# TensorE's work in the order of emission, with estimated pauses between a mixer's steps

## The chip, the cores and the metric

The kernel runs on one core of a Trainium2 chip. The metric is the device time of one execution in microseconds (us), the median of three runs. The engines are TensorE (PE in the rows; its weight loads are PEld), VectorE (DVE), ScalarE (ACT), GpSimd (POOL) and SyncE (SP), which issues the DMAs.

## What is computed

Two sequences of 512 tokens go through two layers of an encoder. In each layer four mixers work side by side on parts of one projection, and their normalised outputs are joined by a second one:

```
def encoder_trunk(x, p):
    for l in range(DEPTH):
        h = rms_norm(x, p['ln1_g'][l]).astype(x.dtype)
        z = h @ p['w_in'][l]
        z_s5, z_hy, z_rw, z_na = jnp.split(z, IN_SPLITS, axis=-1)
        y_s5 = s5_mixer(z_s5, ...)
        y_hy = hyena_mixer(z_hy, ...)
        y_rw = rwkv_mixer(z_rw, ...)
        y_na = na_mixer(z_na, ...)
        groups = [rms_norm(y, p['grp_g'][l, i]).astype(x.dtype) for i, y in enumerate((y_s5, y_hy, y_rw, y_na))]
        x = x + jnp.concatenate(groups, axis=-1) @ p['w_out'][l]
        h = rms_norm(x, p['ln2_g'][l]).astype(x.dtype)
        x = x + jnp.square(jax.nn.relu(h @ p['w_mlp1'][l])) @ p['w_mlp2'][l]
    return x
```

The model width is 1024, the hidden width 4096. S5 is a state-space scan in 16 groups; Hyena is two long convolutions by Fourier transforms (forward products, a product of spectra, inverse products); RWKV is a delta-rule recurrence over both directions, worked in chunks of 64 tokens; the attention looks at 8 rows by 16 columns around each token.

## The kernel before

**Dense products.** A layer l of sequence b has `w_in` (22 tiles of 128 output channels), `w_out` (8), `mlp1` (32) and `mlp2` (64 halves of a tile's sum). Each product is made with its operands split in a high and a low part, as three matmuls of 128x512 columns (`mm3`, L1433 high by high, L1434 high by low, L1435 low by high). One weight piece of 256 KB (4 x 128 x 128) serves 12 matmuls; there are 9024 dense matmuls in all. `load_w` brings a piece: the first time the raw weights come by DMA, ScalarE casts the high part (L300), VectorE subtracts to get the low part (L301, both in `split`), and a DMA stores the low part; for the second sequence high and low come by DMA and ScalarE casts (L1417). There are seven buffers for weight pieces' parts; a first-time piece uses one of three for the high part and one of four for the low.

**Mixers.** Each mixer is a generator that yields between its steps. RWKV has two `rw_step` calls for each (l, b), one for each group of chunks. In each, for the two halves c of the channels, small products (L413) give decay and gate, some twenty elementwise instructions on ScalarE, VectorE and GpSimd make from them the operands of the pair products (L470), whose last ones are L453 and L454. Then come transposes (L506), an inversion on VectorE (L515, L516, L533 to L551), 32-row products (L564, L583), and four tail steps (L640, L650, L661, L676, L678), in which VectorE writes the state `rw_st` and GpSimd multiplies it by the decay into `rw_se` (L668). Hyena has forward products (L1227), a product of spectra on VectorE (L1196 among others) and inverse products (L1277), twice. S5's state products are L959 and L1014. Norms take column sums (L271), a reciprocal root on VectorE and transposes that spread it (L289, L296).

**Order.** `together` steps three generators in turn: the dense stream, the RWKV stream and a first stream for the head, two mixer steps for each dense step. A dense step is one whole tile of 24 matmuls. RWKV and S5 of one (l, b) run side by side, then Hyena and attention. This order of emission gives priorities; a scheduler, which plays the instructions through a timeline of its own, puts them in each engine's order, with the dense products at a lower priority (`OFF_P`). So a mixer's product whose operands are not ready is passed by dense products on TensorE. The mixers of one (l, b) lie beside the dense layers of the one before it. `w_out` of an (l, b) needs all four mixers; in the head, (0, 0) has no earlier layer to run beside. PSUM has 2 banks for dense products (`pd`), 3 for `ra` (RWKV, Hyena), 2 for `ma` and 1 for `nm`.

## Time and profile before

| what | value |
|---|---|
| median of three runs | 3193.9 us (3186.03 to 3196.83) |
| profiled execution | 3182.62 us |
| its span | 3180.8 us |
| TensorE busy | 2964.7 us, 93% of the span |
| VectorE busy | 1935.5 us, 61% |
| ScalarE busy | 1128.3 us, 35% |
| GpSimd busy | 453.6 us, 14% |

Shares are averages over the whole span. A window shows the busy time of each engine and the granted TensorE clock of one stretch. The idle time before a group of instructions tells how long its engine stood still just ahead of them, and the name after `<-` tells what ended the wait.

### The profile page before, as it was taken

How to read it: one execution, taken by the hardware profiler on the slowest of the kernel's cores; microseconds unless marked ns; L12 is line 12 of the kernel's file. 1: busy time of each engine (PE TensorE's matmuls, PEld its weight loads, DVE VectorE, ACT ScalarE, POOL GpSimd, SP SyncE). 2: the span in 40 equal slices, each digit the busy share in tenths (PEclk: the TensorE clock that was granted, in tenths of full speed). 3: DMA queues.
4: the chain of work that ended last, by engine and by line, in shares of the span. 5: the costliest groups of instructions: out<-in, count | busy, mean ns of one | idle time of the engine just before them, and what ended most of it. 6: DMA issues, size and time to landing. Idle time of an engine off the chain costs nothing. (4 is left out here: it accounts for less than half of the span.)

```text
span 3180.8 us, 48627 instructions
## 1 busy us (share of the span) xinstructions
PE 2964.7 (93%) x17328; PEld 2317.7 (73%) x17328; DVE 1935.5 (61%) x3909; ACT 1128.3 (35%) x2080; POOL 453.6 (14%) x411
## 2 busy tenths in 40 slices
PE   7978999899999999999999899988999999799999
PEld 5666776677777867777777677866777777588887
DVE  7987783874874697653844527668547467731223
ACT  4333233443332343244332324333433333343332
POOL 3422210200100022211101002213000001100000
PEclk9988997899999999999999999989999999899999
DMA  7577564464565566774764655666646555466666
GB/s 220 184 228 189 172 188 142 139 169 158 163 194 168 188 204 202 240 236 155 207 174 145 182 169 196 218 200 187 177 139 169 174 178 185 155 215 194 194 192 215
DMA packets 491801, 588.70 MB, mean 185 GB/s; under 512 B 188678, under 2 KB 239494, under 8 KB 490536
## 3 DMA queue, kind: packets, MB, share of 16 engines
q1 hardware_dynamic: 491560, 585.59, 60.1%
q8 instruction: 139, 2.28, 0.3%
q14 instruction: 102, 0.84, 0.1%
HBM read 418.34 MB, written 164.22 MB: 183 GB/s over the span
## 5 line engine op out<-in xcount | busy, mean ns | idle before, releaser
L1433 PE MATMUL pd<-m,m 128*128 128x512 f32 x2984 | 1222.0, 410 | 63.8 <-ACT m L300 23.4
L1435 PE MATMUL pd<-m,m 128*128 128x512 f32 x2984 | 1205.7, 405 | 22.5 <-DMA m<-lo 15.7
L1434 PE MATMUL pd<-m,m 128*128 128x512 f32 x2984 | 1205.8, 404 | 1.6 <-DVE m L301 1.4
L1433 PEld LDWEIGHTS pd<-m,m 128*128 128x128 f32 x2984 | 578.3, 194 | 214.2 <-ACT m L300 27.8
L1435 PEld LDWEIGHTS pd<-m,m 128*128 128x128 f32 x2984 | 577.9, 194 | 166.3 <-DMA m<-lo 19.5
L1434 PEld LDWEIGHTS pd<-m,m 128*128 128x128 f32 x2984 | 579.1, 194 | 131.2 <-issue 8.4
L300 ACT CAST m<-m 128x512 fp32r<-128x512 f32 (+1 forms) x400 | 256.4, 644 | 619.9 <-PE pd L1434 220.6
L1417 ACT CAST m<-m 128x512 fp32r<-128x512 f32 x376 | 232.2, 619 | 612.9 <-DMA m<-in_w_mlp 362.4
L301 DVE TENSOR_TENSOR m<-m,m 128x512 fp32r<-128x512 f32 (+1 forms) x400 | 303.1, 761 | 203.4 <-ACT m L300 198.1
L1596 DVE TENSOR_TENSOR m<-pd,m 128x512 f32<-128x512 f32 x224 | 153.9, 688 | 205.4 <-PE pd L1435 204.5
L1578 DVE SCALAR_TENSOR_TENSOR do<-pd,do 128x512 f32<-128x512 f32 x128 | 88.0, 687 | 202.4 <-ACT do L1577 201.9
L1196 DVE TENSOR_TENSOR m<-m,m 128x512 f32<-128x512 f32 (+1 forms) x224 | 125.6, 601 | 6.5 <-PE ma L1375 4.8
L301 DVE TENSOR_TENSOR m<-do,m 128x512 fp32r<-128x512 f32 x128 | 88.2, 689 | 50.0 <-ACT m L300 49.2
L300 ACT CAST m<-do 128x512 fp32r<-128x512 f32 x128 | 79.4, 621 | 98.7 <-DVE do L1578 98.5
L1577 ACT ACTIVATE do<-pd 128x512 f32<-128x512 f32 x128 | 75.9, 593 | 37.6 <-PE pd L1435 37.3
L668 POOL TENSOR_TENSOR rw_se<-rw_st,rw_ec 128x256 f32<-128x256 f32 x24 | 15.8, 659 | 484.1 <-DVE rw_st L669 361.9
L470 PE MATMUL ra<-m,m 64*128 64x128 f32 x512 | 63.1, 308 | 21.8 <-DVE m L454 10.3
L1196 POOL TENSOR_TENSOR m<-m,m 128x512 f32<-128x512 f32 x32 | 49.0, 1534 | 234.7 <-DVE m L1196 77.7
L1457 POOL TENSOR_TENSOR m<-m 128x512 f32<-128x512 f32 x40 | 59.8, 1494 | 152.9 <-ACT m L1456 150.9
L863 POOL TENSOR_TENSOR m<-m,s5p_i 128x256 f32<-128x256 f32 x64 | 61.7, 963 | 135.7 <-DVE m L865 71.4
L678 PE MATMUL ra<-m,m 128*64 128x64 f32 x512 | 78.8, 248 | 1.3 <-DVE m L653 0.9
L470 PEld LDWEIGHTS ra<-m,m 64*128 64x128 f32 x512 | 54.3, 206 | 34.9 <-issue 24.3
(363 smaller groups left out, 3505.6 us busy)
## 6 DMA issues: line engine op xcount, KB each, us to landing
m<-in_w_mlp SPq DMA_DIRECT2D x512, 256.0 KB, 2.9
lo<-m SPq DMA_DIRECT2D x376, 256.0 KB, 2.6
m<-lo SPq DMA_DIRECT2D x376, 256.0 KB, 2.7
m<-in_w_in SPq DMA_DIRECT2D x176, 256.0 KB, 3.2
m<-zr SPq DMA_DIRECT2D x36, 512.0 KB, 4.8
m<-in_w_out SPq DMA_DIRECT2D x64, 256.0 KB, 3.5
m<-in_xT SPq DMA_DIRECT2D x32, 256.0 KB, 4.3
zr<-do SPq DMA_DIRECT2D x32, 256.0 KB, 2.4
```

The lines of the kernel that those rows point to most:

```text
L300: self.nc.scalar.copy(out=hi, in_=x)
L301: eng.tensor_tensor(out=lo, in0=x, in1=hi.bitcast(F32), op=SUB)
L470: nc.tensor.matmul(out=pm[q][:, ch - c2, c], lhsT=bk[c][h, ch].rearrange("p a b -> p (a b)"), rhs=ar[c][h, ch].rearrange("p a b -> p (a b) ...
L678: nc.tensor.matmul(out=py[b0:b0 + 64, d, c], lhsT=uv[:, ch, c, q], rhs=sr[:, ch, 2 * c + q], start=st is None, stop=True)
L1196: eng.tensor_tensor(out=o, in0=a, in1=b, op=op)
L1417: nc.scalar.copy(out=hi, in_=raw)
L1433: K.nc.tensor.matmul(out=ps, lhsT=wh, rhs=hh, start=(i == 0), stop=False)
L1434: K.nc.tensor.matmul(out=ps, lhsT=wh, rhs=hl, start=False, stop=False)
L1435: K.nc.tensor.matmul(out=ps, lhsT=wl, rhs=hh, start=False, stop=(i == n - 1))
L1577: nc.scalar.activation(out=r, in_=ps, func=AF.Relu)
L1578: nc.vector.scalar_tensor_tensor(out=r, in0=ps, scalar=0.0, in1=r, op0=MAX, op1=MUL)
L1596: nc.vector.tensor_tensor(out=a, in0=ps, in1=a, op=ADD)
```

## The change

All matmuls and transposes go through a helper `K.pe`, which adds an estimated duration to a clock of its own for each. A mixer's `yield N` now says in how many estimated us its next step can begin. `pace` takes the place of `together`: it steps each mixer whose time has come, then one dense step, which is now half a tile (12 matmuls); when nothing moved the clock, it moves it by 0.5. From the first `w_out` on (`(0, 0, "out")`) TensorE executes in the order of emission; the scheduler places the other engines as before. Norms become generators with pauses; the norm of `w_in` and `mlp` is spread between the first dense tiles, whose results wait in PSUM (`early`). RWKV's tail steps, attention's `values` and Hyena's transposes yield more often. Attention starts at the tail of the second `rw_step`, and Hyena right after RWKV, so that three mixers can run at once; their memory may use a further region. Of first-time weights three low parts in four are subtracted on GpSimd. The number of matmuls of each kind stays the same.

```diff
+class PE:
+
+
+    def __init__(self, nc):
+        self.nc, self.clock = nc, 0.0
+
+    def matmul(self, out, lhsT, rhs, **kw):
+        n = int(np.prod(rhs.shape[1:]))
+        self.clock += n * (0.00044 if rhs.dtype == F32R else 0.00168)
+        self.nc.tensor.matmul(out=out, lhsT=lhsT, rhs=rhs, **kw)
+
+    def transpose(self, out, x, eye):
+        self.clock += 0.11
+        self.nc.tensor.transpose(out, x, eye)
...
         if square:
             nc.vector.reciprocal(out=x, in_=x)
-            return x
-        return self.rsqrt(x, n, tag)
-
-    def head_bcast(self, rn, M, tag):
+            y = x
+        else:
+            y = self.rsqrt(x, n, who)
+        yield 4.5
+        return y
+
+    def head_bcast(self, rns, M, tag, use):
 
         nc = self.nc
-        ex = M([P, 4, 2, 64])
-        nc.scalar.copy(out=ex, in_=rn.unsqueeze(3).to_broadcast([P, 4, 2, 64]))
-        pb = self.p([P, S], tag)
-        for q in range(4):
-            nc.tensor.transpose(pb[:, q * P:q * P + P], ex[:, q].rearrange("p a b -> p (a b)"), self.eye)
-        M.free(ex)
-        return pb
+        exs = []
+        for rn in rns:
+            ex = M([P, 4, 2, 64])
+            nc.scalar.copy(out=ex, in_=rn.unsqueeze(3).to_broadcast([P, 4, 2, 64]))
+            exs.append(ex)
+        yield 2.5
+        for c, ex in enumerate(exs):
+            pb = self.p([P, S], tag)
+            for q in range(4):
+                self.pe.transpose(pb[:, q * P:q * P + P], ex[:, q].rearrange("p a b -> p (a b)"), self.eye)
+            use(c, pb)
+            M.free(ex)
...
         bk.append(b_t)
-        yield
+        yield (2, 11)[c]
...
             wt = K.t([P, 2, 2, 64], "rw_wt")
             nc.vector.tensor_tensor(out=wt, in0=pw, in1=wv[:, sl], op=ADD)
+            yield 2
...
         Z = [z0, z1, a, Y[0]]
-        yield
+        yield 9
...
-        values(c, 0, s0, vt)
-        yield
+        yield 9
+        yield from values(c, 0, s0, vt)
         if c == 0:
             a = yield from project(1)
-        values(c, 2, s1, vt)
+        yield 4
+        yield from values(c, 2, s1, vt)
         M.free(vt)
-        yield
+        yield 2
...
-        K.split(hi, lo, raw, nc.vector)
+        K.split(hi, lo, raw, nc.vector if K.nw % LO_V == 0 else nc.gpsimd)
...
 def dense(K, key, h, tag="pd"):
 
-    w = [load_w(K, key + (kh,)) for kh in range(2)]
     ps = K.p([P, S], tag)
-    mm3(K, ps, [(w[k // 4][0][:, k % 4], w[k // 4][1][:, k % 4], h[k][0], h[k][1]) for k in range(8)])
+    for kh in range(2):
+        wh, wl = load_w(K, key + (kh,))
+        mm3(K, ps, [(wh[:, j], wl[:, j]) + h[4 * kh + j] for j in range(4)], kh == 0, kh == 1)
+        if kh == 0:
+            yield
     return ps
...
-def norm_rstd(K, st, M, square=False):
-
-    K.tc.cur_priority -= OFF_R
-    rn = K.token_rstd([st["acc"]], S, K.ones[:, 0:1], 1e-6, "nm", sc=1.0 / D, square=square)
+def norm_rstd(K, st, M, out, square=False):
+
+    yield
+    rn = yield from K.token_rstd([st["acc"]], S, K.ones[:, 0:1], 1e-6, "nm", "nm", sc=1.0 / D, square=square)
     M.free(st['mem'])
     pb = K.p([P, S], "nm")
     K.bcast(rn, pb)
     r = K.t([P, S], "R")
     K.nc.scalar.copy(out=r, in_=pb)
-    K.tc.cur_priority += OFF_R
-    return r
-
-
-def w_in(K, l, par, h, R, dst, tags):
+    out.append(r)
+
+
+def w_in(K, l, par, h, st, M, dst, tags):
 
     nc = K.nc
     zr, zd, zh, zn = dst
+    Rs = []
+    rs = norm_rstd(K, st, M, Rs)
+    next(rs)
...
+    R, early = None, []
     for off, n, fn in ((8, 8, rw), (0, 2, s5), (2, 6, hy), (16, 6, na)):
         for i in range(n):
-            fn(i, dense(K, ('w_in', l, off + i), hp, tags.pop() if tags else "pd"))
+            ps = yield from dense(K, ('w_in', l, off + i), hp, tags.pop() if tags else "pd")
+            if R is None:
+                next(rs, None)
+                early.append((fn, i, ps))
+                if Rs:
+                    R = Rs[0]
+                    for f, j, p in early:
+                        f(j, p)
+            else:
+                fn(i, ps)
             yield
...
-        first(f)
+        yield from first(f)
+        next(rs, None)
         yield
...
-    def __init__(self, gen, n=1, off=0):
-        self.gen, self.n, self.off, self.live = gen, n, off, True
+    def __init__(self, gen):
+        self.gen, self.live, self.ready = gen, True, 0.0
 
     def step(self, K):
-        for _ in range(self.n):
-            if self.live:
-                K.tc.cur_priority += self.off
-                try:
-                    next(self.gen)
-                except StopIteration:
-                    self.live = False
-                K.tc.cur_priority -= self.off
-
-
-def together(K, *streams):
-
-    for _ in both(K, *streams):
-        pass
+        try:
+            self.ready = K.pe.clock + (next(self.gen) or 0.0)
+        except StopIteration:
+            self.live = False
 
 
 def both(K, *streams):
 
     while any(s.live for s in streams):
         for s in streams:
-            s.step(K)
-        yield
+            if s.live and s.ready <= K.pe.clock:
+                s.step(K)
+        yield max(0.0, min([s.ready for s in streams if s.live], default=0.0) - K.pe.clock)
+
+
+def pace(K, dense, ordered, *mixers):
+
+
+    region = None
+    while dense.live or any(s.live for s in mixers):
+        now = K.pe.clock
+        n = 0
+        for s in mixers:
+            if s.live and s.ready <= now:
+                s.step(K)
+                n += 1
+        if dense.live:
+            dense.step(K)
+        if K.pe.clock == now:
+            K.pe.clock += 0.5
+        if region is None and ordered():
+            region = K.tc.manual_schedule(engines={mybir.EngineType.PE})
+            region.__enter__()
+    if region is not None:
+        region.__exit__(None, None, None)
...
-        DM, MX = K.mem((0, DHI)), K.mem((DHI, NMEM))
+        DM, MX, MN = K.mem((0, DHI)), K.mem((DHI, NMEM), (0, DHI)), K.mem((DS5, NMEM), (DHI, DS5), (0, DHI))
         DS, MW = K.mem((0, DLO)), K.mem((DLO, DHI), (DHI, NMEM))
-        MR, MS = K.mem((DHI, DS5), (DS5, NMEM), tight=True), K.mem((DS5, NMEM), (DHI, DS5))
+        MR, MS = K.mem((DHI, DS5), (DS5, NMEM), (0, DHI), tight=True), K.mem((DS5, NMEM), (DHI, DS5), (0, DHI))
...
+                if i >= 15:
                     done.add(("zr", l, b))
-                    if b == 0 and l and len(ys[l - 1, 1]) == 4:
-                        take(l - 1, 1)
-                    if b == 1 and l and len(ys[l, 0]) == 4:
-                        take(l, 0)
+                    other = (l, 0) if b else (l - 1, 1)
+                    if l and len(ys[other]) == 4 and other not in taken:
+                        take(*other)
...
+                done.add((l, b, "out"))
...
-                yield from both(K, Stream(rwkv(l, b, MR)), Stream(chain(until(("z", l, b)), s5(l, b, MS))))
+                K.b = b
+                yield from both(K, Stream(rwkv(l, b, MR)), Stream(chain(
+                    until(("z", l, b), ("ops", l)), s5(l, b, MS), s5_ops(K, 1, MS, "ma") if i == 1 else (),
+                    until(("tail", l, b), ("freed",) + before) if i else (), na(l, b, MN, "ma") if i else ())),
+                    Stream(chain(until(("rw", l, b), ("freed",) + before), hyena(l, b, MX, "ra")) if i else chain()))
                 if i:
-                    yield from until(("freed",) + before)
-                    yield from both(K, Stream(hyena(l, b, MX, "ra")), Stream(na(l, b, MX, "ma")))
                     if i == 1:
-                        yield from prep(1, MX, "ma")
+                        yield from hy_spectra(K, 1, MX, "ma")
...
-        together(K, Stream(first_stream(), FN, OFF_M), Stream(rwkv_stream(), MIX), Stream(ds, 1, OFF_D))
+        pace(K, Stream(ds), lambda: (0, 0, "out") in done, Stream(first_stream()), Stream(rwkv_stream()))
...
-OFF_D, LO_V, MIX = 0, 4, 2
-FN, OFF_M, OFF_W, OFF_P, OFF_R = 2, 0, 0, 2000, 0
+LO_V, OFF_W, OFF_P = 4, 0, 2000
```

`K.mem` with more regions takes the later ones only when the earlier are full. `manual_schedule` fixes the order of the engines it names within its region.

**The end of the mixers on TensorE.** These rows stand ahead of the last `w_out`, in the kernel before; `ra` and `ma` are banks of the mixers, `pd_25377` is the first tile of `w_out`, and the last dense product of the preceding layer stands twelve rows ahead of the first row here, with 28 more L1277 products between.

```order
L1277 MATMUL ra_22905<-m_22100,m_22771 128x128
L1277 MATMUL ra_22916<-m_22100,m_22771 128x128
L296 MATMUL ma_22764<-c_eye_129,rsq_yma_22752 128x128 x4
L271 MATMUL ra_22979<-c_ones_131,m_22974 128x1 x4
L296 MATMUL ra_22998<-c_eye_129,rsq_yra_22986 128x128 x4
L1433 MATMUL pd_25377<-m_25351,m_25365 128x512
```

In the changed kernel the same place, from the last products of the preceding layer (`pd_25309`) to `w_out` (`pd_25367`); L203 is the helper's matmul, L207 its transpose:

```order
L203 MATMUL pd_25309<-m_25022,m_25301 128x512 x2
L203 MATMUL pd_25309<-m_25022,m_25302 128x512
L203 MATMUL pd_25309<-m_25083,m_25301 128x512 x2
L203 MATMUL pd_25309<-m_25083,m_25302 128x512
L203 MATMUL ra_25326<-c_ones_131,m_25244 128x1 x4
L207 MATMUL ra_25346<-c_eye_129,rsq_yra_25333 128x128 x4
L203 MATMUL pd_25367<-m_25353,m_25368 128x512 x2
```

The Hyena inverse (L1277) and the transposes of its neighbour's norm are no longer behind the last dense product; one norm's sums and transposes are.

**RWKV's preparation on TensorE.** In the kernel before, `m_13725` and `m_13726` are the operands of the first half, `m_13769` and `m_13770` those of the second. Between the second half's first products (L413) and these rows stand 20 dense products, three L470 products of the first half, and 35 more dense products, of which the last ones are shown:

```order
L1434 MATMUL pd_17641<-m_14040,m_17629 128x512
L1435 MATMUL pd_17641<-m_14040,m_17630 128x512
L1433 MATMUL pd_17641<-m_14152,m_17629 128x512
L1434 MATMUL pd_17641<-m_14152,m_17629 128x512
L470 MATMUL ra_13831<-m_13769,m_13770 128x128
L470 MATMUL ra_13832<-m_13769,m_13770 128x128
L470 MATMUL ra_13831<-m_13725,m_13726 128x128
L470 MATMUL ra_13832<-m_13725,m_13726 128x128
```

In the changed kernel `m_15277` is an operand of the first half, `m_15345` of the second. Between the second half's L413 products and these stand 48 dense products, of which the last are shown:

```order
L203 MATMUL pd_15401<-m_13823,m_15420 128x512 x2
L203 MATMUL pd_15401<-m_13823,m_15421 128x512
L203 MATMUL pd_15401<-m_13888,m_15420 128x512 x2
L203 MATMUL pd_15401<-m_13888,m_15421 128x512
L203 MATMUL ra_15446<-m_15277,m_15278 128x128
L203 MATMUL ra_15447<-m_15277,m_15278 128x128
L203 MATMUL ra_15446<-m_15345,m_15346 128x128
L203 MATMUL ra_15447<-m_15345,m_15346 128x128
```

The pair products of both halves now come together, with 48 dense products between the second half's first products and them instead of 55.

**The tail of a `rw_step` on GpSimd.** In the kernel before, three `rw_se` stand one behind the other, then come the instructions of the next step:

```order
L668 TENSOR_TENSOR rw_se_20015<-rw_st_19970,rw_ec_19062 128x256
L668 TENSOR_TENSOR rw_se_20109<-rw_st_20013,rw_ec_19062 128x256
L668 TENSOR_TENSOR rw_se_20163<-rw_st_20107,rw_ec_19062 128x256
L430 MEMSET m_20253 128x8x2
L442 TENSOR_TENSOR m_20260<-m_20226,m_20253 128x8x64
```

In the changed kernel L699 is that instruction, and L326 is the subtraction for a weight piece's low part (`m_21130` and so on):

```order
L699 TENSOR_TENSOR rw_se_21099<-rw_st_20974,rw_ec_19276 128x256
L326 TENSOR_TENSOR m_21130<-m_21131,m_21129 128x512
L326 TENSOR_TENSOR m_21172<-m_21173,m_21171 128x512
L699 TENSOR_TENSOR rw_se_21245<-rw_st_21097,rw_ec_19276 128x256
L326 TENSOR_TENSOR m_21276<-m_21277,m_21275 128x512
L326 TENSOR_TENSOR m_21310<-m_21311,m_21309 128x512
L326 TENSOR_TENSOR m_21376<-m_21377,m_21375 128x512
L699 TENSOR_TENSOR rw_se_21408<-rw_st_21243,rw_ec_19276 128x256
```

Between one `rw_se` and the next there now stand two or three subtractions for weights.

## Rows read from the trace of the kernel before

**Rows 1.** The page, busy us of each engine, share of the span, instructions:

```profile
PE 2964.7 (93%) x17328; PEld 2317.7 (73%) x17328; DVE 1935.5 (61%) x3909; ACT 1128.3 (35%) x2080; POOL 453.6 (14%) x411
```

**Rows 2.** Windows: length, busy us (x) of PE, PEld, DVE, ACT, POOL, clock, DMA:

```profile
0.00:590.00 590.00, 524.86 (x3332) 396.31 (x3333) 443.21 (x1001) 211.90 (x395) 150.62 (x146) 0.89 0.63 185
590.00:1420.00 830.00, 774.00 (x4625) 608.15 (x4624) 566.47 (x1125) 301.32 (x560) 128.06 (x115) 0.97 0.62 190
1420.00:2780.00 1360.00, 1271.17 (x7639) 987.83 (x7638) 816.98 (x1629) 479.20 (x896) 168.45 (x146) 0.95 0.58 178
2100.00:2200.00 100.00, 81.23 (x492) 66.33 (x491) 84.66 (x203) 31.20 (x54) 28.89 (x20) 0.85 0.63 199
2700.00:2800.00 100.00, 78.74 (x378) 61.50 (x377) 66.51 (x128) 32.02 (x63) 10.48 (x8) 0.88 0.52 167
2900.00:3000.00 100.00, 100.00 (x441) 82.51 (x440) 25.34 (x39) 32.42 (x55) 0.00 (x0) 1.00 0.61 195
```

**Rows 3.** TensorE's groups by line, 590 to 2780 us: busy, mean ns, idle before:

```profile
L1433 PE MATMUL pd<-m,m 128*128 128x512 f32 x2056 | 845.2, 412 | 41.3 <-DVE do L1578 13.8 <-ACT m L300 6.9 <-ACT m L1417 6.4
...
L470 PE MATMUL ra<-m,m 64*128 64x128 f32 x384 | 48.0, 310 | 19.1 <-DVE m L454 10.3 <-DVE m L453 5.8 <-POOL m L454 2.7
...
L1277 PE MATMUL ra<-m,m 128*128 128x128 f32 x192 | 26.4, 293 | 10.6 <-DVE m L1196 10.5
...
L959 PE MATMUL ma<-m,m 128*64 128x64 f32 x384 | 20.8, 244 | 11.7 <-DMA m<-s_sB 11.7
```

**Rows 4.** TensorE's waits, 590 to 2780 us: total us, times, longest:

```profile
PE ra L564 <- DVE m L551: 18.1, 6, 4.4
```

**Rows 5.** TensorE's timeline at the mixers' end: start, duration, line, [idle before <-releaser]:

```profile
2748.99 0.95 PE L271 MATMUL ma<-c_ones,m 128*128 128x1 f32 x8
2758.25 5.63 PE L1277 MATMUL ra<-m,m 128*128 128x128 f32 x32 [8.31 <-DVE m L1196]
...
2770.18 1.86 PE L271 MATMUL ra<-c_ones,m 128*128 128x1 f32 x8 [5.86 <-DVE m L1534]
2774.18 1.08 PE L296 MATMUL ra<-c_eye,rsq_yra 128*128 128x128 f32 x4 [2.13 <-DVE rsq_yra L257]
2777.92 1.22 PE L1433 MATMUL pd<-m,m 128*128 128x512 f32 x2 [2.65 <-ACT m L300]
```

**Rows 6.** TensorE's timeline, RWKV's first products and pair products, shortest and longest of six:

```profile
1733.78 1.32 PE L413 MATMUL ra<-m 64*128 64x256 f32 x12
...
1750.92 1.57 PE L470 MATMUL ra<-m,m 64*128 64x128 f32 x18 [0.83 <-DVE m L454]
...
2159.28 1.70 PE L413 MATMUL ra<-m 64*128 64x256 f32 x18
...
2187.92 3.47 PE L470 MATMUL ra<-m,m 64*128 64x128 f32 x18 [2.67 <-POOL m L454]
```

**Rows 7.** TensorE's timeline, Hyena's forward products and an inverse:

```profile
2070.27 0.70 PE L1227 MATMUL ra<-m,m 128*128 128x256 f32 x2
...
2120.22 3.10 PE L1277 MATMUL ra<-m,m 128*128 128x128 f32 x24 [1.60 <-DVE m L1196]
...
2716.07 1.13 PE L1227 MATMUL ra<-m,m 128*128 128x256 f32 x4
```

**Rows 8.** Timeline of VectorE and GpSimd, a subtraction with and one without a neighbour:

```profile
617.87 1.47 POOL L1457 TENSOR_TENSOR m<-m 128x512 f32<-128x512 f32 x1 [3.14 <-ACT m L1456]
...
618.16 1.72 DVE L301 TENSOR_TENSOR m<-m,m 128x512 fp32r<-128x512 f32 x1
...
622.73 0.68 DVE L301 TENSOR_TENSOR m<-m,m 128x512 fp32r<-128x512 f32 x1
```

**Rows 9.** GpSimd's waits over the span: total us, times, longest:

```profile
POOL rw_se L668 <- DVE rw_st L669: 361.9, 16, 44.1
```

More of the change, by code (lines that the diff above doesn't have):

```diff
@@ L708, in rw_bonus @@
     yield
+    for c in range(2):
+        p2 = K.p([P, S], "ra")
+        K.pe.matmul(out=p2, lhsT=K.bd, rhs=r[:, c], start=True, stop=True)
+        nc.vector.tensor_tensor(out=r[:, c], in0=p2, in1=v[:, c], op=MUL)
+    M.free(v)
+    yield
     gate = M([P, 2, S])
@@ L740, in rw_out @@
         nc.vector.tensor_tensor(out=y[:, c], in0=gate[:, c], in1=y[:, c], op=MUL)
-        yield
+    rv = rn.rearrange("p (a b c) -> p a b c", a=4, b=2)
+    yield from K.head_bcast([rv[:, :, c] for c in range(2)], M, "ra", finish)
     M.free(bonus, gate)
+    yield 4
 def s5_ops(K, l, M, tag):
@@ L979, in s5_front @@
         M.free(tb, *t)
-        for _ in range(2):
-            yield
+        yield 4
     t = M([P, 8, 128])
@@ L1090, in hy_spectra @@
     for i, w in ((0, w1), (1, w2)):
+        yield 4
         pm = K.p([64, S], tag)
-        nc.tensor.matmul(out=pm, lhsT=w, rhs=h, start=True, stop=True)
+        K.pe.matmul(out=pm, lhsT=w, rhs=h, start=True, stop=True)
         M.free(h)
@@ L1747, in end @@
                     h2.append(norm_split(K, t, pars[l + 1], 'ln1_g', m, st2, DM))
-            yield from mlp(K, l, h, R2, xm, end, DM)
+            yield from mlp(K, l, h, st, xm, end, DM)
             if not last:
```

252 lines of the change are left out of this document (133 added, 119 removed).

## Prediction

> **What bounds the kernel now.** I read the page's busy shares first, then the windows, then the idle time of TensorE by what ended it, last single places in its timeline. TensorE is busy for 93% of the span [rows 1], so time can only come from its idle time and its clock. In the pure dense stretch of 2900 to 3000 us it never stops, the granted clock is 1.00 (the upper of its two levels, 2.4 GHz), and 441 products take 100 us: 0.227 us for a 128x512 dense product [rows 2]. 9024 such products are 2048 us; the rest are the mixers' small products and the waits.
>
> From 590 to 1420 us TensorE idles 830 - 774.0 = 56 us, from 1420 to 2780 us 1360 - 1271.2 = 89 us [rows 2]: 145 us between them. In that stretch the idle time stands before the dense products (L1433, 41.3 us), RWKV's pair products (L470, 19.1), the S5 products (L959, 11.7) and the Hyena inverse (L1277, 10.6) [rows 3], and before RWKV's L564 (18.1) [rows 4]. The waits are short and many, the releaser is mostly VectorE, which is busy for 61% of the span [rows 1]. Where they gather, the clock falls as well: 0.85 in 2100 to 2200 us and 0.88 in 2700 to 2800 us [rows 2], which is to say that TensorE ran at the lower level (1.2 GHz) for part of it; 15 + 12 = 27 us of clock are lost in these two windows.
>
> The profiled execution took 3182.6 us, 11.3 below the median of the runs. I make the sum against 3182.6 and add 11.3 at the end. A measurement of this kernel tells about 0.3% (9.6 us) from no change.
>
> **The change, part by part.** The number of matmuls of each kind stays as it is. What moves is the order on TensorE, from the first w_out on, and one elementwise kind from VectorE to GpSimd.
>
> (a) *End of the mixers.* After the last dense product of the preceding layer comes the second Hyena inverse with nothing beside it: from 2749.94 (2748.99 + 0.95) to 2777.92 us no dense product runs, 28.0 us [rows 5]. In the new order the Hyena products stand before the last 60 dense products (13.6 us), and only four column sums and four transposes stay behind them. What is left is half of the 1.86 for the sums, the 2.13 wait, 1.08 and the last wait of 2.65: 6.8 us [rows 5]. The 6.3 us between the inverse's end (2758.25 + 5.63) and the sums (2770.18) then lie beside those 13.6. Gain 21 us; it is 0 if the dense stream comes to its end before the Hyena does, as it does now.
>
> (b) *L564 (RWKV's 32-row products).* The wait is 18.1 us in six places, 3 each [rows 4]. The new order puts 216 to 264 dense products (49 to 60 us) between the L506 transposes and L564, where there are 164 to 223 now (37 to 51). That is 9 us or more in each place against 3 us of wait. Gain 18; what comes next there, the L583 products, follows after a yield of 2.5 and has 12 dense products (2.7 us) beside it.
>
> (c) *S5 (L959).* Each step now has 12 dense products between it and the next; the 11.7 us of waits are all for a DMA [rows 3], which is issued by then. I take 8 of them; 0 to 11.7.
>
> (d) *Dense products themselves.* L1433 waits for 41.3 us for casts and activations [rows 3]. Chains between dense products keep their order, but the norm's sums and broadcasts now lie between the next layer's first tiles, which wait in PSUM. From 0 (the same casts are late) to 41; I take 20.
>
> (e) *Clock.* Of the 27 us [rows 2] 20 come back if (a) and the small waits go; 0 to 27.
>
> (f) *RWKV's preparation, a loss.* Between the second half's first products (L413) and the pair products (L470) that need both halves, the new order has exactly 48 dense products in all six places, 10.9 us. In the trace that distance is 15.8 us at the shortest (1735.10 to 1750.92) and 26.95 at the longest (2160.97 to 2187.92), and both end in a wait for the last elementwise product [rows 6]. With their mean of 21.4 the new stall is 10.5 us in each place, 63 in all, where there are 19.1 now [rows 3]: +44. But VectorE's queue between those products is shorter in the new order: 26 to 40 instructions where there were 27 to 52, by the trace's durations about a fifth less. A fifth off 21.4 leaves 17.1, a stall of 6.2, 37 in all: +18. I take 18; the ends are -19 and +44.
>
> (g) *Hyena, from its forward products (L1227) to its inverse (L1277), a loss.* The new order puts 120 to 144 dense products there, 27 to 33 us, about 30. The trace has 49.25 us (2070.97 to 2120.22) and 41.05 (2717.20 to 2758.25), both ending in a wait for VectorE [rows 5, 7]. At 45 and three places that is 15 short each, +45; if VectorE's own work there sets it, which no longer competes with a second mixer's, 0. I take +15.
>
> (h) *The head.* Up to the first w_out the scheduler still sets TensorE's order, but the steps come in another order and finer. The head idles 590 - 524.9 = 65 us at a clock of 0.89 [rows 2]. I see no reason for a gain: ahead of the first w_out no dense products are left, and RWKV, Hyena and attention have only each other for cover, now with more steps and more waits between them. +8, from -20 to +45.
>
> (i) *Low parts on GpSimd.* 282 of the 376 subtractions for first-time weights move. VectorE saves 0.68 us each, 192 us; GpSimd takes about 1.47 us for the same shape [rows 8]. The two engines get into each other's way: while GpSimd ran for 1.47 us, VectorE's subtraction took 1.72 instead of 0.68 [rows 8], 1.04 more. If VectorE meets that as often as it is busy, 61% [rows 1], it loses 282 x 1.04 x 0.61 = 179 us of the 192. So 0. The Trainium skill, "SBUF — State Buffer", section "Who interferes with whom", speaks against this move: the port that the two share is an exclusive lock, and a VectorE instruction with two SBUF inputs waits for the whole of a GpSimd instruction that reads SBUF. The 1.72 agrees with that.
>
> Sum: -21 - 18 - 8 - 20 - 20 + 18 + 15 + 8 + 0 = -46. 3182.6 - 46 + 11.3 = 3148 us, 1.4% faster. With (d), (e) and the losses between nearer bounds it is 3100 to 3184.
>
> **Rivals.**
> *The chains are longer than their cover (slower).* VectorE's time at (f) and (g) stays as it is: +44 and +45. Each stall stops TensorE for 10 us or more, as the end of the mixers does now; then none of the 27 us of clock comes back and as much again is lost. -21 - 18 - 8 - 20 + 44 + 45 + 8 + 27 = +57: 3251. It decides from some 60 us of stalls at L470 and L1277 above today's. For it speaks that waits are left there [rows 6, 7] although the scheduler had put 55 dense products ahead of the second half's L470 in one such place, seven more than now; against it the shorter queue.
>
> *Most waits go.* An order with enough between the steps takes all 145 us and the 27 us of clock: 3182.6 - 172 + 11.3 = 3022. Against it: (f) and (g).
>
> *The waits only change places.* The 9024 dense products are all the cover there is; what (b) gets is taken from (f) and (g). Gains and losses balance: about 3194. This is also what it gives if the other engines, still placed by the scheduler, keep TensorE to the old rhythm.
>
> *GpSimd blocks VectorE in full.* Each of the 282 holds VectorE for 1.47 us: 415 - 192 = +223 us of VectorE time, 7% of the span. It reaches TensorE only where TensorE waits for VectorE: six times 21.4 and three times 45 are 263 us, 7% of that is 18. 3148 + 18 = 3166. The rule of the Trainium skill named in (i) would give this if VectorE always had a two-input instruction waiting; the 1.72 bears it out for one such pair.
>
> *The low parts stand behind RWKV's state in GpSimd's queue (slower).* L668 waits there for VectorE, 361.9 us in 16 times, 22.6 in the mean and 44.1 at the longest [rows 9]. The new order has two or three subtractions between one such instruction and the next. Four buffers of low parts cover 4 x 12 x 0.227 = 10.9 us; the 11.7 beyond stop TensorE at, say, the 12 of 24 that lie among first-time weights: +140, 3288. Against it: RWKV's tail steps now follow each other with 2.7 us of dense work between, and the waits get shorter as the instruction is issued later.
>
> **How the numbers follow.** Forecast (3148, within 3100 to 3184) 0.38; most waits go (3022) 0.12; full block (3166) 0.08; places only (3194) 0.13; chains too long (3251) 0.21; GpSimd's queue (3288) 0.08. Faster by over 0.3% (below 3184.3): 0.38 + 0.12 + 0.08 = 0.58; within it 0.13; slower 0.29. The range leaves out the queue's case and half of the best one, with a little over: 3045 to 3262; the likeliest case alone has 3100 to 3184.
>
> **What would show it.** (a) right: under 10 us without a dense product ahead of the last w_out. (b) right: next to no idle time before the successor of L564. (f), (g): the idle time before the successors of L470 and L1277, 37 and some 25 us; over 60 and 45 the slower rival holds. (e): a granted clock above 0.95 in each 100 us around w_out of the second layer. (i): the duration of VectorE's two-input instructions while GpSimd subtracts, and of the waits for a low part. It is wrong altogether if the idle time before dense products grows, since no term has a price for that, or if the head's 590 us change by over 45.

## The result and the profile after

The changed kernel is slower: 3330.4 us median against 3190.0 for the kernel before, a ratio of 1.044 with the interval 1.039 to 1.049. The prediction was 3148 us, within 3045 to 3262; the time lies outside, on the other side.

| | before | after |
|---|---|---|
| median of four runs | 3189.97 us | 3330.43 us |
| span of the profiled execution | 3180.8 us | 3327.1 us |
| TensorE busy | 2964.7 us | 2993.2 us |
| TensorE idle (span less busy) | 216 us | 334 us |
| mean granted clock | 0.949 | 0.926 |

The page's busy line after, which answers to [rows 1]:

```profile
PE 2993.2 (90%) x17328; PEld 2321.7 (70%) x17328; DVE 1875.6 (56%) x3627; ACT 1136.8 (34%) x2084; POOL 814.8 (24%) x693
```

The span grew by 146 us: 118 of idle time and 28 of busy time for the same instructions, while the mean granted clock fell. VectorE's busy time fell by 60 us and GpSimd's rose by 361.

Windows of after (length, busy us and instructions of PE, PEld, DVE, ACT, POOL, clock, DMA share, GB/s): the head and the beginning of the first `w_out`, the rest up to 1420 us, and the stretch around the last mixers' end. They answer to [rows 2].

```profile
0.00:600.00 600.00, 509.74 (x3252) 377.73 (x3252) 428.73 (x932) 207.55 (x385) 193.66 (x179) 0.88 0.61 177
600.00:700.00 100.00, 65.02 (x408) 50.91 (x407) 77.29 (x204) 23.86 (x40) 20.00 (x18) 0.71 0.36 108
700.00:1420.00 720.00, 644.91 (x3808) 495.94 (x3807) 441.88 (x781) 255.91 (x477) 267.66 (x223) 0.93 0.56 170
2828.00:2979.00 151.00, 131.18 (x584) 107.85 (x583) 87.02 (x131) 47.09 (x77) 35.72 (x26) 0.92 0.65 205
```

In 600 to 700 us TensorE works for 65.0 us only, at a clock of 0.71. Up to 1420 us in all it idles 90 + 35 + 75 = 200 us; the kernel before idles 121 there [rows 2], but has got further by that time: the trace of after passes the 3056th of the 9024 dense products at 1404 us, that of before at 1266. At the 4050th it is 211 us behind, and from there to the end it makes up some 65 of them: its mixers' products have taken 538 us of TensorE by then, those of the kernel before 471. (Places in the dense stream are counted over all 9024 products here; the ones that two expectations below call the 1002nd and the 5514th are the 1066th and the 5542nd.)

TensorE's waits after (total us, times, longest), where every matmul has line 203 and every transpose 207; they answer to [rows 3, 4]:

```profile
PE ma L203 <- DMA m<-s_sB: 36.6, 11, 12.7
PE pd L203 <- ACT m L325: 31.7, 11, 12.9
PE ra L203 <- DVE m L482: 21.4, 5, 6.2
PE pd L203 <- DVE do L1648: 18.2, 11, 4.1
PE pd L203 <- DVE m L1515: 16.6, 8, 4.2
PE pd L203 <- DVE m L1666: 16.5, 7, 5.9
...
PE ra L203 <- DVE m L481: 11.1, 3, 5.4
...
PE ma L203 <- DMA m<-s_sC: 10.9, 7, 4.7
PE pd L203 <- POOL m L326: 8.9, 12, 1.6
...
PE ra L203 <- DVE m L578: 0.6, 1, 0.6
```

L481 and L482 are the last elementwise products of RWKV's preparation (before: L453, L454), L578 is what L564's wait ended in (before: L551), `s_sB` and `s_sC` are S5's operands, L325 is the cast of a weight piece's high part and L326 the subtraction of its low part. The largest line is S5's `s_sB`: 36.6 us in 11 times, where [rows 3] had 11.7.

The longest of these, in TensorE's timeline of after:

```profile
641.36 0.98 PE L203 MATMUL ra<-m 64*128 64x256 f32 x12
655.03 1.12 PE L203 MATMUL ma<-m,m 128*64 128x64 f32 x16 [12.69 <-DMA m<-s_sB]
656.08 7.75 PE L203 MATMUL pd<-m,m 128*128 128x512 f32 x24
669.42 1.12 PE L203 MATMUL ma<-m,m 128*64 128x64 f32 x16 [5.59 <-DMA m<-s_sB]
```

and SyncE's queue at the same time:

```profile
651.71 0.32 SPq L989 DMA_DIRECT2D m<-s_tb  x1
652.21 0.32 SPq L987 DMA_DIRECT2D m<-s_sB  x1
```

with VectorE's last instruction on the preceding group, and SyncE's waits for that instruction and for L1011, one of the same group, over the span (total us, times, longest):

```profile
651.56 0.61 DVE L1015 TENSOR_TENSOR m<-m,m 128x64 f32<-128x64 f32 x4
```

```profile
SPq L989 <- DVE m L1011: 38.4, 15, 11.8
...
SPq L987 <- DVE m L1015: 16.1, 2, 9.7
```

The S5 products stand at the head of TensorE's queue for 12.69 us. Their operand's DMA is issued only at 652.21, when VectorE is done with L1015 (651.56 + 0.61). Behind them stand 24 dense products of `w_out` which then run without a wait of their own. In a fixed order they can't pass.

The end of the mixers, which answers to [rows 5]:

```profile
2896.52 13.86 PE L203 MATMUL pd<-m,m 128*128 128x512 f32 x60
2910.22 0.95 PE L203 MATMUL ra<-c_ones,m 128*128 128x1 f32 x8
2918.41 1.09 PE L207 MATMUL ra<-c_eye,rsq_yra 128*128 128x128 f32 x4 [7.25 <-DVE rsq_yra L274]
2922.15 0.79 PE L203 MATMUL pd<-m,m 128*128 128x512 f32 x1 [2.65 <-ACT m L325]
```

Between the last dense product of the preceding layer (2896.52 + 13.86) and `w_out` there are now 11.8 us instead of 28.0.

### The profile page after: what moved, and what is told of

It is laid out like the page before. It is cut to its first block, busy times and chain, and to the rows that moved or that the text cites. A ratio compares the mean times of both kernels' runs of the same rounds, so it can differ in the third digit from the quotient of the medians.

```text
span 3327.1 us, 48633 instructions
## 1 busy us (share of the span) xinstructions
PE 2993.2 (90%) x17328; PEld 2321.7 (70%) x17328; DVE 1875.6 (56%) x3627; ACT 1136.8 (34%) x2084; POOL 814.8 (24%) x693
## 5 line engine op out<-in xcount | busy, mean ns | idle before, releaser
L203 PE MATMUL pd<-m,m 128*128 128x512 f32 x8952 | 2280.1, 411 | 136.9 <-ACT m L325 31.7
L203 PEld LDWEIGHTS pd<-m,m 128*128 128x128 f32 x8952 | 1722.9, 197 | 575.7 <-issue 66.0
L326 POOL TENSOR_TENSOR m<-m,m 128x512 fp32r<-128x512 f32 x282 | 389.3, 1382 | 773.1 <-ACT m L325 727.9
L325 ACT CAST m<-m 128x512 fp32r<-128x512 f32 (+1 forms) x400 | 257.5, 645 | 742.0 <-PE pd L203 353.8
L203 PE MATMUL ra<-m,m 32*32 32x32 f32 (+5 forms) x3448 | 266.0, 247 | 45.1 <-DVE m L482 21.4
L203 PEld LDWEIGHTS ra<-m,m 32*32 32x32 f32 (+4 forms) x3448 | 200.1, 147 | 109.1 <-issue 58.7
L203 PE MATMUL ma<-m,m 128*64 128x128 f32 (+10 forms) x1584 | 194.5, 318 | 88.3 <-DMA m<-s_sB 36.6
L203 PEld LDWEIGHTS ma<-m,m 128*64 128x64 f32 (+4 forms) x1584 | 116.1, 157 | 142.4 <-issue 54.3
L326 DVE TENSOR_TENSOR m<-m,m 128x512 fp32r<-128x512 f32 (+1 forms) x118 | 100.3, 850 | 106.5 <-ACT m L325 106.2
L326 DVE TENSOR_TENSOR m<-do,m 128x512 fp32r<-128x512 f32 x128 | 91.5, 715 | 63.8 <-ACT m L325 63.4
L325 ACT CAST m<-do 128x512 fp32r<-128x512 f32 x128 | 79.6, 622 | 109.9 <-DVE do L1648 109.7
L1515 DVE SCALAR_TENSOR_TENSOR m<-m,par,m 128x512 fp32r<-128x512 f32 x64 | 62.9, 993 | 39.3 <-ACT m L1514 39.3
L203 PE MATMUL ra<-m,rw_st 64*64 64x64 f32 x448 | 74.5, 248 | 0.0
L560 DVE TENSOR_TENSOR m<-m 128x1024 f32<-128x1024 f32 x32 | 64.6, 2019 | 14.7 <-DMA m<-m 8.2
```

Source lines behind the costliest of these rows:

```text
L203: self.nc.tensor.matmul(out=out, lhsT=lhsT, rhs=rhs, **kw)
L325: self.nc.scalar.copy(out=hi, in_=x)
L326: eng.tensor_tensor(out=lo, in0=x, in1=hi.bitcast(F32), op=SUB)
L560: nc.vector.tensor_tensor(out=tm, in0=x[:, i:i + 4].unsqueeze(2).to_broadcast([P, 4, 16, 16]), in1=z.rearrange("p j k -> p k j").unsqueeze ...
L1515: nc.vector.scalar_tensor_tensor(out=h[:, 1], in0=x, scalar=g, in1=h[:, 0].bitcast(F32), op0=MUL, op1=SUB)
```

## The experiments

On the chips of the experiments the kernel before took 3182 to 3187 us, so the changed one stands at some 3324 (1.0441 times as much). Ratios are against the kernel before. The changed kernel wasn't measured again beside the experiments, so a difference from its 3324 carries both intervals, some 18 to 20 us: 89 and 44 us are clear of that, 25 us only just. Busy and idle time are those of one profiled execution each, which doesn't lie at its kernel's median (e12's by 18.5 above it, e2's by 13 and e5's by 9 below).

| kernel | median us | ratio (interval) | TensorE busy, idle us |
|---|---|---|---|
| before | 3182 to 3187 | 1 | 2965, 216 |
| changed | 3330 | 1.044 (1.039 to 1.049) | 2993, 334 |
| e1_sched: no fixed order | 3235 | 1.017 (1.012 to 1.021) | 2979, 255 |
| e2_dve: low parts on VectorE | 3280 | 1.030 (1.026 to 1.034) | 2972, 293 |
| e5_sched_dve: both | 3188 | 1.002 (0.999 to 1.004) | 2964, 214 |
| e4_before_pool: before, low parts on GpSimd | 3209 | 1.008 (1.005 to 1.012) | 2981, 227 |
| e3_s5: longer pauses in S5 | 3299 | 1.037 (1.033 to 1.041) | 2988, 302 |
| e6_rw22: longer pause in RWKV | 3299 | 1.036 (1.033 to 1.039) | 2977, 312 |
| e11_scale125: all pauses x 1.25 | 3289 | 1.033 (1.030 to 1.036) | 2968, 317 |
| e7_scale16: all pauses x 1.6 | 3438 | 1.079 (1.077 to 1.082) | 3030, 401 |
| e8_headzero: no pauses in the head | 3298 | 1.036 (1.033 to 1.039) | 2975, 318 |
| e10_fixed_dve_head_s5_rw: fixed order, four repairs | 3249 | 1.019 (1.015 to 1.022) | 2944, 308 |
| e9_sched_dve_head: scheduler, VectorE, no pauses in the head | 3156 | 0.990 (0.987 to 0.993) | 2951, 208 |
| e12_sched_dve_nopause: the same, no pauses at all | 3178 | 0.998 (0.996 to 0.999) | 2968, 227 |

Three theories stood against each other: A, the fixed order stops TensorE wherever an estimate is too short; B, the low parts on GpSimd slow the weights and VectorE; C, the head alone lost the time.

**The fixed order, and the low parts: e1, e2, e5 and e4.** e1 never opens the region of the fixed order:

```diff
-        if region is None and ordered():
+        if False and region is None and ordered():
```

> The changed kernel with everything but the fixed order: the scheduler places TensorE's instructions too, from the same finer steps and pauses. Theory A (TensorE waits in a fixed order wherever an estimated pause is shorter than the work of the other engines) says that most of the 140 us comes back: 3190 to 3230 us, with the mixers' S5 and RWKV waits down to the level of the kernel before. Theory B (the low parts on GpSimd, and the store of each low part that SyncE's queue waits for, delay the weights and slow VectorE) says 3310 to 3340, as the changed kernel. Theory C (the head alone, where the scheduler sets the order in both kernels, lost 50 to 80 us to the new order of emission) says 3240 to 3290.

e2 puts all low parts back on VectorE:

```diff
-        K.split(hi, lo, raw, nc.vector if K.nw % LO_V == 0 else nc.gpsimd)
+        K.split(hi, lo, raw, nc.vector)
```

> The changed kernel with all low parts on VectorE again. Theory A: within 20 us of the changed kernel's 3330, since VectorE gets back what GpSimd gave (VectorE busy from 1876 to some 1950 us). Theory B: 3200 to 3250. The prediction's own price for the move was 0.

e5 is both edits at once:

> The changed kernel without the fixed order and with all low parts on VectorE: what stays are the finer steps, the pauses and the new overlap of three mixers. If order and low parts add up (the fixed order cost some 90 us by the first of these runs, the low parts 28 to 45), it takes 3190 to 3207 us. If the low parts on GpSimd only hurt through the fixed order, 3225 to 3240; they did cost 28 us in the kernel before, so I expect the first. Anything left above 3182 is the price of the steps themselves, above all in the head.

e4 is the kernel before with the one line of the change:

```diff
-        K.split(hi, lo, raw, nc.vector)
+        K.split(hi, lo, raw, nc.vector if K.nw % LO_V == 0 else nc.gpsimd)
```

> The kernel before with three in four low parts on GpSimd and nothing else. Theory A: within 20 us of 3190. Theory B: 3270 to 3330.

Without the fixed order the time falls by 3324 - 3235 = 89 us, with the low parts on VectorE by 44, with both by 136: they add up, and nothing is left above the kernel before (ratio 1.002). Each price comes out the same with and without the other: from e2 to e5 the order's is 92 us, from e1 to e5 that of the low parts 47. e1 came out 5 us above theory A's range and below C's as a number; by its ratio it is 3243 on the scale of the first result, inside C's. e5 then showed that what e1 had left was the low parts. e2 lies between A and B, which means that both hold, A for two thirds and B for one. e4's 3209 is inside A's range as a number, but the kernel before took 3182 beside it: 27 us, B's direction, and less than B alone had asked for.

The S5 and RWKV waits of e1 (total us, times, longest):

```profile
PE ra L203 <- DVE m L481: 9.4, 4, 3.7
...
PE ma L203 <- DMA m<-s_sB: 5.5, 7, 1.4
...
PE ma L203 <- DMA m<-s_sC: 3.3, 5, 1.5
...
PE ra L203 <- DVE m L482: 3.0, 3, 2.2
```

The scheduler places the same steps from the same emission, and `s_sB` costs 5.5 us instead of 36.6, RWKV's two products 12.4 instead of 32.5. So it isn't the finer steps that wait; it is that in the fixed order nothing passes them. Over all places the order's price stands ahead of the mixers' products: there TensorE idles 334 - 137 = 197 us in the changed kernel and 255 - 140 = 115 in e1, while the idle time ahead of dense products hardly differs (136.9 and 139.7).

What the move to GpSimd did to the two engines can be read from the busy lines, e4 against [rows 1] first, and from GpSimd's own group in e4 (busy us, mean ns, idle before):

```profile
PE 2980.7 (93%) x17328; PEld 2319.1 (72%) x17328; DVE 1871.5 (58%) x3627; ACT 1127.4 (35%) x2080; POOL 829.5 (26%) x693
```

```profile
L301 POOL TENSOR_TENSOR m<-m,m 128x512 fp32r<-128x512 f32 x282 | 395.4, 1405 | 765.5 <-ACT m L300 694.4 <-DMA m<-rw_D 23.8 <-issue 16.9
```

282 subtractions at the mean of 0.73 us that VectorE took for them before (274.0 us for 376, the row below) are 206 us, but VectorE's busy time fell by 64 only (1935.5 to 1871.5). The other 142 us, 0.50 for each subtraction of 1.405, are VectorE's own other instructions getting longer beside GpSimd: in e4's trace those that overlap one of the 282 take 136 us more than the same instructions do when GpSimd is idle. The row of the kernel before:

```profile
L301 DVE TENSOR_TENSOR m<-m,m 128x512 fp32r<-128x512 f32 x376 | 274.0, 731 | 183.4 <-ACT m L300 178.3 <-DMA zn<-do 2.1 <-DMA lo<-m 1.7
```

Which instructions get longer can be read from VectorE and GpSimd in e4, side by side:

```profile
1286.28 0.48 DVE L865 TENSOR_TENSOR m<-m,m 128x128 f32<-128x128 f32 x2
...
1287.67 1.28 POOL L301 TENSOR_TENSOR m<-m,m 128x512 fp32r<-128x512 f32 x1
1287.74 1.56 DVE L865 TENSOR_TENSOR m<-m,m 128x128 f32<-128x128 f32 x2 [0.51 <-POOL m L863]
...
2504.43 1.29 POOL L301 TENSOR_TENSOR m<-m,m 128x512 fp32r<-128x512 f32 x1 [1.41 <-ACT m L300]
2504.96 0.69 DVE L1578 SCALAR_TENSOR_TENSOR do<-pd,do 128x512 f32<-128x512 f32 x1 [3.09 <-ACT do L1577]
```

L865 has both inputs in SBUF. Two of them take 0.48 us alone and 1.56 beside the subtraction, and the first ends 0.15 us after the subtraction does. L1578 has one of its inputs in PSUM (`pd`): the 40 that overlap a subtraction take 0.69 us in the mean, as those that don't.

TensorE waits for a low part that GpSimd makes for 8.9 us only in the changed kernel. But in e4, where nothing else was changed, the idle time ahead of dense products rose from 87.9 us to 138.4, as far as in the changed kernel; the largest of its three groups, which had 63.8 us:

```profile
L1433 PE MATMUL pd<-m,m 128*128 128x512 f32 x2984 | 1227.8, 412 | 110.0 <-ACT m L300 36.3 <-ACT m L1417 20.8 <-DVE m L1596 15.9
```

So the dense products wait more for casts and for VectorE. TensorE's whole idle time rose by 11 us only, as that ahead of the mixers' products fell, and its busy time by 16. Through which chain the low parts cost their time wasn't separated by any run.

**Pauses: e3, e6, e11 and e7.** e3 lengthens S5's pauses:

```diff
         M.free(tb, *t)
-        yield 4
+        yield 12
...
             M.free(Cop)
-            yield 1
+            yield 5
```

> The changed kernel with longer pauses in S5 alone: 12 instead of 4 after each group of the front, 5 instead of 1 after each group of the back. The front's products wait for 36.6 us for their DMA and the back's for 10.9 us in the changed kernel. Theory A: these waits fall below 15 us in all and the time by 25 to 45 us, to 3285 to 3305; if the clock comes back with them, by more. Theory B: no more than 10 us.

e6 lengthens the one ahead of RWKV's pair products:

```diff
-        yield (2, 11)[c]
+        yield (2, 22)[c]
```

> The changed kernel with the pause ahead of RWKV's pair products 22 instead of 11, so some 96 instead of 48 dense products stand there. Theory A as the prediction's term (f) has it: the waits of 32.5 us for the two last elementwise products fall below 8 and the time by 20 to 30 us, to 3292 to 3302 on the scale of these runs, on which the changed kernel takes some 3322. Rival (the waits only change places): the waits there fall, others grow by as much, and the time stays within 10 us of 3322.

Each gives 25 us, only just clear of the interval. In e3 no wait for `s_sB` is left among TensorE's waits, but those for L481 and L482 rose from 32.5 to 39.8. In e6 the RWKV waits fell to 10.0 us, the S5 waits stayed in sum (46.1 us, 47.5 in the changed kernel):

```profile
PE ma L203 <- DMA m<-s_sB: 26.8, 9, 12.9
PE ma L203 <- DMA m<-s_sC: 19.3, 13, 4.1
...
PE ra L203 <- DVE m L481: 8.1, 1, 8.1
...
PE ra L203 <- DVE m L482: 1.9, 1, 1.9
```

So these estimates were too short, as theory A has it. e11 and e7 multiply all pauses:

```diff
-            self.ready = K.pe.clock + (next(self.gen) or 0.0)
+            self.ready = K.pe.clock + 1.25 * (next(self.gen) or 0.0)
```

(1.6 in e7.)

> The changed kernel with every pause 1.25 times as long; 1.6 times gave 3438. With 1.6 the trace was 147 us ahead at the 5514th dense product and lost 283 us in the two stretches ahead of the last two w_out, where the mixers ended without dense products. If that is a matter of running out of cover, 1.25 gives a smaller share of both: 3290 to 3360, ahead of the changed kernel in the middle and with a loss in the stretch ahead of the last w_out alone. If the estimates were simply too short, 3270 to 3300.

> The changed kernel with every pause of a mixer 1.6 times as long. Theory A (the estimates are too short): TensorE's idle time, 334 us of the span in the changed kernel, falls by 60 to 100 and the time to 3220 to 3270. Rival (the dense products are all the cover there is, and mixers that end later stand bare ahead of w_out): idle time ahead of w_out grows, 3310 to 3360.

1.25 gives 35 us, just under the first reading's range and inside the second's; by the time alone the second fits better. 1.6 costs 114 us, more than the rival had allowed for. Windows of e7 show where (columns as above): the stretch ahead of the second layer's first `w_out` and what follows, and that ahead of the last one.

```profile
1516.00:2145.00 629.00, 585.68 (x3392) 456.55 (x3391) 287.18 (x540) 213.70 (x382) 59.83 (x53) 0.95 0.64 190
2145.00:2465.00 320.00, 242.27 (x1399) 188.25 (x1398) 209.91 (x451) 97.33 (x187) 81.89 (x71) 0.81 0.44 133
2774.00:3083.00 309.00, 237.89 (x1399) 186.26 (x1398) 155.05 (x311) 83.13 (x169) 49.98 (x44) 0.80 0.39 129
```

From 1516 to 2145 us TensorE idles 629 - 585.7 = 43 us. Then it idles 78 and 71 us in two stretches of some 310, at clocks of 0.81 and 0.80: the dense products are used up there and the mixers, started later, stand bare (136 and 129 us pass between two dense products; ahead of the last `w_out` it was 11.8 in the changed kernel). e11 has the same place in small, as the first reading said: it comes to the stretch before the last `w_out` 125 us ahead of the changed kernel and takes 85 us longer for it. Longer pauses are worth something only as long as dense products are left to fill them.

**The head: e8, e9 and e12.** e8 takes all pauses as zero until the first `w_out`:

```diff
-            self.ready = K.pe.clock + (next(self.gen) or 0.0)
+            wait = next(self.gen) or 0.0
+            self.ready = K.pe.clock + (wait if (0, 0, "out") in K.done else 0.0)
```

> The changed kernel with all pauses taken as zero until the first w_out, so that in the head, where the scheduler sets TensorE's order, the mixers' steps are emitted one for each half tile as they come. Theory C (the pauses let the dense steps run ahead in emission and with them the head loses its cover): the first w_out begins near 550 us as before instead of near 600, and the time falls by 30 to 50 us, to 3270 to 3290. If the head's loss comes from the low parts on GpSimd instead, it stays within 10 us of 3322.

The first `w_out` begins at 569 us instead of 601, and its tenth product, the 1066th dense one, comes at 589, 45 us earlier than in the changed kernel. But the time falls by 26, since the last mixers' end takes 76 us more, with some 49 us more of mixers' products, which the changed kernel has behind it by then, and some 30 us more of idle time. Part of the head's loss was the pauses', and half of the gain was given back later. e9 is the same head with the scheduler and with VectorE's low parts:

> No fixed order, low parts on VectorE, and the pauses of the mixers taken as zero until the first w_out. With the pauses in the head the same kernel took 3188 us and reached the 1002nd dense product at 586 us, 32 us later than the kernel before, but lost none of it in the end. If the head's loss is the pauses' alone and the rest stays, 3150 to 3165 us, faster than both kernels. Rival (what the head gains is given back where the last mixers end, as with the fixed order, where the head came 45 us earlier and the time fell by 24): 3175 to 3190.

3156 us, ratio 0.990: inside the first reading's range, and faster than both kernels. Against e5 that is 32 us, so the pauses in the head cost that, although e5 as a whole is level with the kernel before: gains elsewhere had paid for it. Only 13 of the 32 stand in the head as idle time (up to the 1080th dense product TensorE idles 73.6 us in e9 and 86.8 in e5). e9 too gives back a good part of its lead, 54 us against e5 where the last mixers end, so that isn't a matter of the fixed order.

e12 leaves out all pauses:

> As the fastest so far (no fixed order, low parts on VectorE), but with no pauses anywhere: each mixer's step is emitted at every half tile. If the pauses do nothing once the scheduler places TensorE's instructions, 3145 to 3170 us, as with zero pauses in the head alone (3156). If the mixers, emitted earlier, take PSUM banks and memory ahead of their time, or if the last mixers end earlier and the end of the dense products gets longer, it moves by over 20 us either way.

3178: 22 us more than e9, just over the bound that I had set. The pauses behind the head do something even where the scheduler places TensorE: without them RWKV's inversion is waited for again,

```profile
PE ra L203 <- DVE m L578: 28.5, 5, 12.7
```

28.5 us against 1.4 in e9 and 20.8 over the span of the kernel before. But all the pauses together, the head's too, do harm there: e5, which has them, took 3188 us, 10 more than e12. How much the finer steps and the three mixers at once are worth by themselves was tested by no run.

**All repairs with the fixed order: e10** (VectorE, no pauses in the head, e3's and e6's pauses).

> The fixed order with all that has helped it one by one: low parts on VectorE (-42), zero pauses in the head (-24), longer pauses in S5 (-23) and ahead of RWKV's pair products (-23), from some 3322. If they add up, 3210 us. If each of them draws on the same dense products, so that longer pauses take cover from one another, 3235 to 3270. The fixed order stays slower than the kernel before in either case.

3249: they don't add up (75 us instead of 120). TensorE's waits in e10:

```profile
PE ma L207 <- DVE rsq_yma L274: 36.8, 3, 14.3
...
PE ma L203 <- DMA m<-s_sB: 24.0, 3, 18.8
PE ra L203 <- DVE m L1236: 22.3, 3, 18.8
...
PE ra L203 <- DVE m L482: 2.4, 2, 1.6
```

RWKV's waits are all but gone, but the norm's root and the Hyena spectra are waited for now, and S5's operand still, by up to 18.8 us at a time. Ahead of the last `w_out` 98 us pass without a dense product, 11.8 in the changed kernel. The time lies in the range of the second reading, and this place fits it: what one place gets in cover, another lacks.

## Why the prediction was wrong, point by point

- **(a), the end of the mixers: right in mechanism, over-sized.** 28.0 us became 11.8, a gain of 16 where 21 was foreseen; the prediction's own sign, under 10, was missed. The 60 dense products didn't quite cover the chain behind the Hyena: 7.25 us of wait were left ahead of the transposes, where the sum had 2.13.
- **(b), L564: right.** 18.1 became 0.6 us.
- **(c), S5: wrong, and by sign.** The sum took 8 us of gain from 12 dense products between the steps. But the DMA was not issued by then: SyncE stands for VectorE's last instructions on the preceding group (38.4 and 16.1 us) before it issues the next group's DMAs, so a step lasts as long as VectorE's queue and the DMA together. The two S5 lines went from 11.7 and 2.1 to 36.6 and 10.9 us. e3 took it away and got 25 us.
- **(d), dense products: wrong.** The forecast gave back 20 us; the idle time ahead of dense products rose from 88 us over the span (63.8, 1.6 and 22.5 in the kernel before's groups) to 136.9 in after's one group (busy us, mean ns, idle before):

```profile
L1433 PE MATMUL pd<-m,m 128*128 128x512 f32 x2984 | 1222.0, 410 | 63.8 <-ACT m L300 23.4
L1435 PE MATMUL pd<-m,m 128*128 128x512 f32 x2984 | 1205.7, 405 | 22.5 <-DMA m<-lo 15.7
L1434 PE MATMUL pd<-m,m 128*128 128x512 f32 x2984 | 1205.8, 404 | 1.6 <-DVE m L301 1.4
```

```profile
L203 PE MATMUL pd<-m,m 128*128 128x512 f32 x8952 | 2280.1, 411 | 136.9 <-ACT m L325 31.7
```

  The prediction had said that it would be wrong if this grew, and had no price for it. The rise isn't the order's: it is there without the fixed order (139.7 in e1) and with GpSimd's subtractions alone (138.4 in e4), and is smaller where VectorE makes the low parts (120.3 in e2, 115.9 in e5). It goes with (i), and for the 28 us that e5 has left with the new steps.
- **(e), the clock: wrong, and by sign.** 20 us were to come back; TensorE's busy time rose by 28 with the same instructions, and the clock fell to 0.71 where the waits gather. It was to be above 0.95 around `w_out` of the second layer and is 0.88 in 2300 to 2400 us. By and large the runs with more idle time have the lower mean clock (0.950 at 208 us in e9, 0.905 at 401 in e7), so it had the sign of (c) and (d). That the 28 us are the clock alone isn't shown: e10 has 2944 us of busy time at 0.937, less than the kernel before at 0.949.
- **(f), RWKV's preparation: right.** 32.5 us of waits, 37 foreseen; 19.1 before. 26.8 of them stand in five of the six places of the sum, 4.9 to 6.2 each where 6.2 was foreseen; the sixth, beside S5's wait of 12.69, has none, and the other 5.7 are in the head.
- **(g), the Hyena: no loss where 15 was foreseen.** No wait for the spectra is left among TensorE's waits, where there were 10.6 us [rows 3]. It came up in e10, with 22.3 us.
- **(h), the head: mis-sized.** +8 was taken, with +45 as the end. The 1066th dense product came at 635 us instead of 554, with 40 us more idle time up to it, and 39 us of mixers' products that moved ahead. It is past the 45 that the prediction had set as a sign of being wrong altogether. Two causes share the idle time. Up to the 1080th it is 65.1 us before and 104.5 after; without the pauses in the head (e8) it is 83.5, with the low parts on VectorE (e2) 88.6, with both and the scheduler (e9) 73.6. The fixed order has next to no part in it (101.5 in e1). The step that failed is that pauses in a part whose order the scheduler sets looked harmless, and that (i) was priced at 0 there too. That pauses do harm because they move a mixer's step back in emission, and so in priority, is an explanation that no run tested.
- **(i), low parts: the mechanism was right, the loss on VectorE over-sized and the conclusion wrong.** 179 of 192 us were to be lost again on VectorE; it was 142 of 206. By the Trainium skill, "SBUF — State Buffer", section "Who interferes with whom", a VectorE instruction with two inputs in SBUF contends with a GpSimd instruction that reads SBUF, for a shared pair of ports that is an exclusive lock. The trace of e4 agrees: L865 above, issued second, ends 0.15 us after the subtraction, while L1578, with one input in PSUM, isn't lengthened. Since only some of the instructions beside a subtraction have two inputs in SBUF, the mean is 0.50 us and not 1.405. But a balance on VectorE isn't the time: the price, put at 0, was 44 us in the changed kernel and 27 in the one before.

From 3148 to 3330 are 182 us. 136 of them are two things that the sum had at nothing, the order and the low parts; the other 46 are the gain that it foresaw, and that the new steps don't bring under the scheduler either (e5 is level with the kernel before).

The step that decided is the one that the sum didn't have: **the price of the order being fixed**, 89 us by e1. The sum went through places of which I could read the cover from the order, and gave each its own wait. In a fixed order every step of every mixer is such a place, with a chance of being late by a few us, and a late one holds the dense products behind it, which the kernel before lets pass. The rival for this (3251) had the mechanism, chains longer than their cover, but not the places: the 60 us above the kernel before that it asked for at L470 and L1277 weren't reached (32.5 and 0 us, against 19.1 and 10.6), and it left out S5 and the norms. The rival of GpSimd's queue had a wrong place: `rw_se` waited less than before,

```profile
POOL rw_se L699 <- DVE rw_st L700: 125.0, 12, 73.3
```

against 361.9 us [rows 9].

## What to carry to other kernels

An order that is fixed in advance has to be right at every step; a scheduler that lets ready work pass needs estimates only as priorities. The estimates cost 2.8% of the time as an order (e1). Given to the scheduler, those behind the head were worth 0.7% (e12 to e9), while all of them together, the head's too, cost some 0.3% (e12 to e5). Pauses take their cover from a stock, here the dense products: add up what all of them ask for before lengthening any. And work moved to a second engine that shares a path with the first has to be priced by the waits that it lengthens, not by what the first engine's busy time loses: here that fell by 64 us and the time rose by 27 (e4).

## What was new about the hardware

A GpSimd subtraction of 128x512 (1.38 to 1.41 us in the mean) lengthens what VectorE does beside it by 0.50 us in the mean, so that of 206 us taken off VectorE 64 were left as a saving. It does so where VectorE's instruction has both inputs in SBUF (0.28 us became up to 1.38 for L865) and not where one is in PSUM (0.69 us either way for L1578). And a stretch of short waits costs more than the waits: in 600 to 700 us of the changed kernel 35 us of idle time went with a clock of 0.71, against 1.00 where dense products run without a stop [rows 2]. The 24 dense products behind S5's wait took 7.75 us, 0.32 each; the 60 ahead of the mixers' end took 13.86, 0.23 each.
